# Delays in a planner's order: key turns, a block's loads, and one product of a two-layer encoder

## The chip, the cores and the metric

The kernel runs on one core of a Trainium2 chip. The metric is the device time of one execution in microseconds (us), and versions are compared by the median of several executions. The engines are TensorE (PE, with its weight loads, PEld, beside it), VectorE (DVE), ScalarE (ACT), GpSimd (POOL) and the queue engine SyncE (SP), which issues nearly all transfers between HBM and the on-chip memory.

## The reference

Two groups of 512 tokens of width 1024 go through the same two layers, each added to its input, and a last normalization. Shortened:

```python
def trunk(x):
    x = x + diff_attention(rms_norm(x, norm_g[0]))    # 8 heads, two softmaxes each
    x = x + bidir_retention(rms_norm(x, norm_g[1]))   # 8 heads, forward and backward
    return rms_norm(x, final_norm_g)

def diff_attention(h):
    q, k, v, gate = split(h @ w_in)                   # 1024 x 8192
    q, k = rotary_half(q) * d ** -0.5, rotary_half(k)
    p = softmax(q @ k.T)                              # two per head
    o = (p[0] - lam * p[1]) @ v
    return (rms_norm(o, subln_g) * (1 - lambda_init) * silu(gate)) @ w_out

def bidir_retention(h):
    q, k, v, gate = split(h @ w_in)                   # 1024 x 6144
    q, k = retention_rotate(q), retention_rotate(k) * dk ** -0.5
    o = retention(q, k, v, g_fwd) + flip(retention(flip(q), flip(k), flip(v), g_bwd))
    return (rms_norm(o, subln_g) * silu(gate)) @ w_out
```

## The kernel before

**Stages.** The order of the work is: input norms and operands; the products of the first layer's input projection; attention, head by head and group by group, with the output projection in between; the second layer's norm and input projection (about 1038 to 1535 us of the profile); retention with its output projection and the last norm (to the end). Each matrix product is split into a high and a low part of fp32r and done in three passes (`PASSES`). Projections go to DRAM and are read back as whole blocks by the stage that follows.

**The projection's products.** The projections use seven products for each 2 x 2 block of a matrix, P1 to P7, in the order P1, P2, P5, P6, P3, P7, P4. A `Unit` is a set of columns with its seven products. For units of kind "pair" (queries, keys, gates) a product is one piece of work of 12 matmuls with 512 columns; for "wide" units (values) it is four pieces of 12 matmuls with 256 columns. P1 of the next unit comes between P7 and P4 of a unit. In the very last unit P4 is the last product of the projection; before it come P4 of the unit before and P7. `projections` is a generator, and `step(proj, n)` lets it add n more products. The right-hand operands of the products lie in slots (`B_SLOT`) that later stages take over: T3 (slots 20 to 23, used by P7) and T4 (24 to 27, used by P4) become the x tiles `xN` of the first and of the second group.

**Turns.** In the second layer's key units (four of them, two heads each) the rotated keys are also needed transposed. `turn`, called from `rot_done`, does it for each of the two groups and for i = 0, 1: four PE transposes into the only PSUM bank of the tag "tp" (line 685), and two DVE multiplications by the decay powers out of that bank (line 688). The first set (i = 0) reads the difference that line 670 makes, the second (i = 1) the sum of line 672. That is four sets a unit, sixteen in all. The turned keys go to DRAM as `kt_d`.

**Retention.** A block is a head and a group. `fetch2(b)` loads a block's queries and keys, values, turned keys and gate. `score2` makes two chunks' scores (line 1221), `state2` a chunk's state (line 1244), `av2` the sums of scores with values (line 1263) and of queries with states (line 1267); after a norm on ACT and POOL comes `turn_o` (line 786) and `gate_o` (line 792). `ahead(b, n)` gives the four pieces state, score, state, score of a block; those of block b + 1 are listed beside the sums of block b. `out_step` is the output projection (line 860) with its addition to x (line 865), and for the last head `final_norm`: a square for the row's norm (`square`, line 883), a multiplication by the gain (line 1285), and, once the row's factor is there (`row_norm`, lines 890 to 893), a scaling (lines 1292 and 1293) and a store.

**The planner.** All of this only lists operations, each with its engine, an estimated cost and what it reads and writes. `Plan.arrange` then simulates the engines and fixes the order of every engine's instructions; the instructions carry no times. An operation becomes known when its predecessors have started or ended (`preds` count to the end, `order` to the start). On PE the operation with the smallest `place` among those that are ready goes next, as long as it is at most `WINDOW` = 24 places ahead of the first one that is not done; on other engines the one with the smallest `late`, the time by which its followers want it. Loads are held back until 15 us before their lateness (`AHEAD`). An issue of a DMA costs 0.5 us in the model. `Plan.issue` runs this three times, each time with the PE starts of the time before, and keeps the order with the shortest span. The parameter `wait` of an operation adds to its place on PE: the transposes of `turn` have 4.

```python
        place = {n: i + ops[n][7] for i, n in enumerate(pe)}
...
        def known(n):
            for e in ops[n][0]:
                heapq.heappush(soon[e], (ready[n], n))
```

Of the kernel before, what the change touches and what calls it, by code (L numbers as in the profile page):

```python
# [15 lines left out]
P = 128  # L16
# [5 lines left out]
NG = 2  # L22
# [44 lines left out]
class Plan:  # L67
# [2 lines left out]

    WINDOW = 24
    AFTER = dict(PE=0.2, DVE=0.12, ACT=0.13, POOL=0.13, SP=0.0)
    SAME = dict(PE=0.0, DVE=.11, ACT=.11, POOL=0.0, SP=0.0)
    BUS = 380.0
    AHEAD = 15.0

    def __init__(self):
        self.rings, self.state, self.ops = {}, {}, []

    def op(self, eng, cost, fn, r=(), w=(), lands=0.0, kb=0, load=False, wait=0):  # L80

        n = len(self.ops)
        costs = eng if isinstance(eng, dict) else {eng: cost}
        preds, order = set(), set()
        for keys, writes in ((r, False), (w, True)):
            keys = [key if isinstance(key, tuple) else (key, None) for key in keys]
            keys += [(k.also, part) for k, part in keys if isinstance(k, Buf) and k.also]
            for thing, part in keys:  # L90
                parts = self.state.setdefault(id(thing), {"thing": thing})
                if isinstance(thing, Buf):
                    if thing.nth + thing.bufs < len(thing.ring):
                        late = thing.ring[thing.nth + thing.bufs]
                        assert late.first is None, f"{thing.tag} {thing.nth} is used after its place was taken"
                    if thing.first is None:
                        assert writes, f"{thing.tag} is read before it is written"
                        thing.first = n
                        if thing.nth:
                            before = thing.ring[thing.nth - 1].first  # L100
                            assert before is not None, f"{thing.tag}: places are taken out of turn"
                            order.add(before)
                        if thing.nth >= thing.bufs:
                            preds.update(thing.ring[thing.nth - thing.bufs].users)
                    elif thing.first != n:
                        order.add(thing.first)
                    thing.users.append(n)
                for q, entry in parts.items():
                    if q == "thing" or not (part is None or q is None or q == part):
                        continue  # L110
                    if entry[0] is not None:
                        preds.add(entry[0])
                    if writes:
                        preds.update(entry[1])
                if writes:
                    if part is None:
                        for q in [q for q in parts if q != "thing"]:
                            del parts[q]
                    parts[part] = [n, []]
                else:  # L120
                    parts.setdefault(part, [None, []])[1].append(n)
        preds.discard(n)
        order -= preds
        self.ops.append((costs, fn, sorted(preds), sorted(order), lands, kb, load, wait))
        return n

    def arrange(self, starts):
# [20 lines left out]
            at = min(recent[n] + 20.0, now + 10.0) if at is None else at - cost  # L148
            late[n] = min(at, starts[n]) if "PE" in costs else at
        pe = [n for n in range(n_ops) if "PE" in ops[n][0]]  # L150
        place = {n: i + ops[n][7] for i, n in enumerate(pe)}
        left = [len(op[2]) + len(op[3]) for op in ops]
        ready = [0.0] * n_ops
        done = [False] * n_ops
# [7 lines left out]

        def known(n):
            for e in ops[n][0]:
                heapq.heappush(soon[e], (ready[n], n))

        for n in range(n_ops):
            if not left[n]:
# [74 lines left out]
def trunk_kernel(  # L243
# [104 lines left out]
    def run(gen):  # L348
        for _ in gen:
            pass  # L350
# [6 lines left out]
    def act(n, fn, r, w):  # L357
        plan.op("ACT", 0.1 + 0.00083 * n, fn, r, w)

    def dve(n, fn, r, w):  # L360
        plan.op("DVE", 0.07 + 0.00104 * n, fn, r, w)

    def pool(n, fn, r, w):
        plan.op("POOL", 0.15 + 0.0024 * n, fn, r, w)
# [7 lines left out]
                nc.vector.tensor_scalar(out(), src(), scale(), None, op0=ALU.mult)  # L372
        plan.op(dict(DVE=0.07 + each * n, ACT=0.1 + 0.00092 * n), 0, fn, r, w)

    def pe(cost, fn, r, w, wait=0):
        plan.op("PE", cost, fn, r, w, wait=wait)

    def dma(out, in_, r, w, kb, eng=None):

        q = eng or nc.sync  # L380
        plan.op("SP" if eng is None else "ACT", 0.5, lambda: q.dma_start(out(), in_()), r, w, lands=2.0 + kb / 200.0,
                kb=kb, load=any(isinstance(k[0] if isinstance(k, tuple) else k, Buf) for k in w))

    def hi_of(n, dst, src, r, w):
# [247 lines left out]
    def rot_done(dst, tab, scaled, turned=None):  # L632
# [44 lines left out]
        def turn(g, *r):  # L677
            h, to = turned
            out = [m_t("kt"), m_t("kt")]
            for i in range(2):  # L680
                tp = bank("tp", "ktp")

                def fn(i=i, tp=tp):
                    for t in range(NT):
                        nc.tensor.transpose(tp[:, t * P:(t + 1) * P], r[i][:, t * P:(t + 1) * P], ident.t)
                pe(0.44, fn, [r[i], ident], [tp], 4)
                for j in range(2):
                    dve(256, lambda i=i, j=j, tp=tp: nc.vector.tensor_tensor(
                        out[j].t.rearrange("p (t i c) -> p t i c", t=NT, i=2)[:, :, i, :],
                        tp.t.rearrange("p (t j c) -> p t j c", t=NT, j=2)[:, :, j, :],  # L690
                        powers[:, 0, h + j, :].unsqueeze(2).broadcast_to([P, NT, 64]), op=ALU.mult),
                        [tp, powers], [(out[j], i)])
            for j in range(2):
                o, k = os_t(), out[j]
                hi_of(S, lambda o=o, k=k: o[:, 0, :], lambda k=k: k.t, [k], [(o, 0)])
                lo_of(S, lambda o=o: o[:, 1, :], lambda k=k: k.t, lambda o=o: o[:, 0, :], [k, (o, 0)], [(o, 1)])
                dma(lambda j=j: to[h + j, g].rearrange("a p c -> p a c"), lambda o=o: o.t.bitcast(F32),
                    [o], [to[h + j, g]], 512)
# [126 lines left out]
            if len(todo) > lag:  # L825
                todo.pop(0)()

    def new_xN(src):
        for g in range(NG):
            for t in range(NT):  # L830
                x = xN[g, t] = slot(20 + 4 * g + t, [P, D], F32)
                dma(lambda x=x: x.t, lambda g=g, t=t: src(g, t)[0], src(g, t)[1], [x], 512)

    def out_weights(w, h, i):
        r = raw_t([P, 2, S])
# [309 lines left out]
    for i in range(N + 3):  # L1145
        at(scores, i, N)
        at(row_max, i, N)
        at(exps, i, N)
        at(combine, i, N)
        if i < 3:  # L1150
            step(proj, 1)
        if i == 2:
            run(proj)
            new_xN(lambda g, t: (xs[g][0, t * P:(t + 1) * P, :], []))
        fill(1, LAG)
        at(transp, i - 1, N)
        fill(1, LAG)
        at(turned, i - 3, N)
        at(av, i - 2, N)
        if i < N and i % 4 == 2 and i > 4:  # L1160
            nh, ng = tiles[i][0:2]
            if ng == 1 and nh + 1 < NH:
                fetch1(nh + 1, 0)
            elif ng == 0 and nh > 0:
                fetch1(nh, 1)
# [19 lines left out]
    def fetch2(b):  # L1185
        h, g = blocks[b]
        for which in range(2):
            qk[b, which] = load_qk((qk_d[1, which, h - h % 2, g], h % 2), (4, 14)[which] + b % 2, (16, 32)[which])
        vt[b] = load_v(v_d[1, h, g], 2 * (b % 2), 0)
        t = kts[b] = slot(6 + b % 2, [P, 2, S], F32R, 16)  # L1190
        dma(lambda: t.t.bitcast(F32), lambda: kt_d[h, g].rearrange("a p c -> p a c"), [kt_d[h, g]], [t], 512)
        sg[b] = load_sg(g_d[1, h, g])

    def decay(h):

# [82 lines left out]
    def final_norm(g, t, i, half, n, key, end):  # L1278
# [3 lines left out]
        if c0 == 0:  # L1282
            zs.append(e_t("z"))
        z = zs[-1]
        dve(n, lambda: nc.vector.tensor_tensor(z[:, c0:c0 + n], half, fin[i][:, c0:c0 + n], op=ALU.mult),
            [key, fin[i]], [(z, c0)])
        if not end:
            return
        r = row_norm(g, t)
        for i, z in enumerate(zs):  # L1290
            plan.op(dict(DVE=0.07 + 0.00058 * S, ACT=0.1 + 0.00092 * S), 0, lambda e, z=z: (
                nc.scalar.activation(z.t, z.t, AF.Copy, scale=r.t) if e == "ACT" else
                nc.vector.tensor_scalar(z.t, z.t, r.t, None, op0=ALU.mult)), [z, r], [z])
            dma(lambda i=i: ys[g][0, t * P:(t + 1) * P, i * S:(i + 1) * S], lambda z=z: z.t, [z], [], 256,
                nc.scalar if n < S and i == 0 else None)
        zs.clear()
# [4 lines left out]

        (state2 if n % 2 == 0 else score2)(b, (1, 0, 0, 1)[n])

    fetch2(0)
    fetch2(1)
    decay(0)
    fin = [const([P, S], n) for n in ("cos", "sin")]
    for i in range(2):
# [5 lines left out]
    N2 = len(tiles2)  # L1314
    wsn.clear()
    owed.clear()
    for j in range(NT):
        ahead(0, j)
        step(proj, 1)
    new_xN(lambda g, t: (x_d[g, t][:], [x_d[g, t]]))  # L1320
    for i in range(N2 + 2):
        if i < N2:
            b, t = tiles2[i]
# [3 lines left out]
                ahead(b + 1, t)  # L1327
            fill(1, LAG)
            av2(b, t)
            if t == 3 and b + 2 < NB:  # L1330
                fetch2(b + 2)
        fill(1, LAG)
# [67 lines left out]
```

## Time and profile before

| | |
|---|---|
| Time, median of 3 runs | 1845.91 us (1844.75 to 1852.18) |
| Time of the profiled execution | 1847.08 us |
| Its span, first to last instruction | 1845.3 us |
| PE busy | 1810.7 us, 98% of the span |
| PEld, DVE, ACT, POOL busy | 1573.3, 1465.4, 955.7, 144.7 us |
| Mean DMA rate | 175 GB/s |

A row of the timeline has the start and the duration in us, engine, line and operation, the tiles written and read, the shape, the count of like instructions merged into it and, in brackets, how long the engine was idle before it and for whom it waited. A row of the waits has the waiting engine, tile and line, whom it waited for, the total in us, the number of times and the longest. A row of a group has its busy time and the mean of one instruction in ns. "q" behind an engine's name is its queue or sequencer. A PE matmul's end is modelled, since matmuls overlap.

### The profile page before, as it was taken

What the parts mean: (1) busy time and instruction counts of PE and PEld (TensorE: products, weight loads), DVE (VectorE), ACT (ScalarE), POOL (GpSimd) and SP (SyncE); (2) the same over time, 40 slices, a digit from 0 to 9 for tenths busy, and PEclk for the clock granted to TensorE, in tenths of its full rate; (3) what the DMA queues carried; (4) which work ended last, traced back from release to release, by engine and by line L of the source; (5) the groups of instructions that cost most, each with busy time, mean ns of one, the idle gap of its engine ahead of it and who ended that gap; (6) DMA issues with size and microseconds to landing.
All of it is one profiled execution on the core that took longest, in us unless ns stands there. A gap on an engine that the chain in (4) does not pass through costs nothing.

```text
span 1845.3 us, 28198 instructions
## 1 busy us (share of the span) xinstructions
PE 1810.7 (98%) x10407; PEld 1573.3 (85%) x10407; DVE 1465.4 (79%) x2514; ACT 955.7 (52%) x1999; POOL 144.7 (8%) x373
## 2 busy tenths in 40 slices
PE   7999999999999999999999999999999999999998
PEld 5789889898898888888888888989898888888887
DVE  7986878887877788888888897868786867777778
ACT  7734434433443565555555874444444446555556
POOL 1000000000000011111111200000000001111112
PEclk9999999999999999999999999999999999999999
DMA  4365536454544684444453434646355559556462
GB/s 161 104 184 158 149 106 219 137 170 151 170 138 160 235 302 164 179 183 164 164 177 124 160 105 136 217 145 192 132 187 167 172 193 367 204 195 228 179 221 92
DMA packets 158547, 322.56 MB, mean 175 GB/s; under 512 B 12597, under 2 KB 72649, under 8 KB 158409
## 3 DMA queue, kind: packets, MB, share of 16 engines
q1 hardware_dynamic: 158080, 320.43, 51.7%
q8 instruction: 81, 1.33, 0.3%
q14 instruction: 58, 0.47, 0.1%
q10 hardware_dynamic: 328, 0.34, 0.1%
HBM read 203.28 MB, written 117.44 MB: 174 GB/s over the span
## 4 chain that ended last, share of the span: by engine, by line
PE 86%; DVE 7%; DMA 4%; ACT 1%; issue 1%; SPq 1%; POOL 0%; POOLq 0%; DVEq 0%; ACTq 0%
PE pj L576 20%; PE pj L860 18%; PE sc L576 10%; PE pj L583 8%; PE o L576 5%; PE o L1108 5%; PE sc L1056 5%; PE sc L583 4%; PE o L1263 2%; PE tp L1092 1%; PE o L786 1%; DMA raw<-in_ret_w_in_dram 1%; DVE ws L388 1%; PE o L583 1%; PE sc L1221 1%
## 5 line engine op out<-in xcount | busy, mean ns | idle before, releaser
L860 PE MATMUL pj<-ws,arena 128*128 128x512 f32 x1542 | 401.7, 398 | 0.3 <-ACT m L370 0.3
L860 PEld LDWEIGHTS pj<-ws,arena 128*128 128x128 f32 x1542 | 275.5, 188 | 49.7 <-ACT m L370 0.5
L576 PE MATMUL pj<-b,ws 128*128 128x512 f32 x1200 | 294.3, 392 | 1.5 <-DVE e L613 1.1
L576 PEld LDWEIGHTS pj<-b,ws 128*128 128x128 f32 x1200 | 224.5, 188 | 50.9 <-issue 1.5
L576 PE MATMUL sc<-arena,ws 128*128 128x512 f32 x960 | 232.3, 392 | 1.1 <-DVE arena L444 1.1
L576 PEld LDWEIGHTS sc<-arena,ws 128*128 128x128 f32 x960 | 180.2, 188 | 40.6 <-DVE arena L444 1.3
L865 DVE TENSOR_TENSOR b<-pj,b 128x512 f32<-128x512 f32 (+1 forms) x257 | 175.8, 684 | 49.0 <-PE pj L860 48.5
L388 DVE TENSOR_TENSOR ws<-st,ws 128x512 fp32r<-128x512 f32 (+1 forms) x192 | 147.7, 774 | 73.2 <-ACT ws L385 60.4
L388 DVE TENSOR_TENSOR ws<-raw,ws 128x512 fp32r<-128x512 f32 (+1 forms) x172 | 147.0, 860 | 73.5 <-ACT ws L385 58.7
L385 ACT CAST ws<-st 128x512 fp32r<-128x512 f32 (+1 forms) x192 | 132.1, 692 | 133.1 <-PE pj L576 39.3
L576 PE MATMUL pj<-arena,ws 128*128 128x512 f32 x720 | 177.3, 392 | 0.0
L385 ACT CAST ws<-raw 128x512 fp32r<-128x512 f32 (+1 forms) x172 | 130.7, 766 | 69.6 <-PE o L576 38.3
L770 POOL TENSOR_SCALAR css<-css 128x1 f32<-128x1 f32 x128 | 32.5, 254 | 1630.3 <-ACT o L768 916.3
L576 PEld LDWEIGHTS pj<-arena,ws 128*128 128x128 f32 x720 | 134.6, 188 | 28.9
L605 ACT COPY c<-pj 128x512 f32<-128x512 f32 x112 | 65.3, 584 | 132.8 <-PE pj L576 87.9
L576 PE MATMUL o<-arena,ws 128*128 128x512 f32 x480 | 117.5, 396 | 1.8 <-DVE e L444 1.8
L583 PE MATMUL pj<-ws,b 128*128 128x256 f32 x960 | 116.9, 276 | 0.0
L583 PEld LDWEIGHTS pj<-ws,b 128*128 128x128 f32 x960 | 113.2, 188 | 0.7
L576 PEld LDWEIGHTS o<-arena,ws 128*128 128x128 f32 x480 | 90.6, 190 | 21.5 <-ACT ws L385 2.0
L1072 ACT ACTIVATE b<-sc,nm 128x512 f32<-128x512 f32 x128 | 87.8, 687 | 39.9 <-DVE nm L1064 39.8
L385 ACT CAST arena<-og 128x256 fp32r<-128x256 f32 x128 | 51.8, 405 | 105.7 <-DVE og L792 105.7
L1108 PE MATMUL o<-arena 128*128 128x256 f32 x768 | 106.1, 288 | 0.0
(176 smaller groups left out, 3000.3 us busy)
## 6 DMA issues: line engine op xcount, KB each, us to landing
qk<-os SPq DMA_DIRECT2D x192, 256.0 KB, 3.8
arena<-qk SPq DMA_DIRECT2D x96, 512.0 KB, 6.2
raw<-in_da_w_in_dram SPq DMA_DIRECT2D x64, 512.0 KB, 5.0
v<-os SPq DMA_DIRECT2D x64, 512.0 KB, 4.8
arena<-v SPq DMA_DIRECT2D x64, 512.0 KB, 4.1
raw<-in_ret_w_in_dram SPq DMA_DIRECT2D x48, 512.0 KB, 4.6
os<-g SPq DMA_DIRECT2D x32, 512.0 KB, 8.6
g<-e SPq DMA_DIRECT2D x48, 256.0 KB, 4.9
```

Source lines behind the costliest of these rows:

```text
L385: act(n, lambda: nc.scalar.copy(dst(), src()), r, w)
L388: dve(n, lambda: nc.vector.tensor_tensor(dst(), src(), hi().bitcast(F32), op=ALU.subtract), r, w)
L576: nc.tensor.matmul(ps.t, a[u][0]()[:, k, :], bt[k][:, v, :], start=(opens and k == 0 and i == 0), stop=(k == 3 and i == 2), skip_group_che ...
L583: nc.tensor.matmul(ps[:, (t % 2) * 256:(t % 2) * 256 + 256], bt[k][:, v, t * P:(t + 1) * P], a[u][0]()[:, k, :], start=(opens and t % 2 == ...
L605: act(S, lambda c=c, ps=ps: nc.scalar.copy(c.t, ps.t), [ps], [c])
L770: pool(60, lambda: nc.gpsimd.tensor_scalar(ss.t, ss.t, 256 * SUB_EPS, None, op0=ALU.add), [ss], [ss])
L860: nc.tensor.matmul(ps[:, here], o[a][:, e, t * P:(t + 1) * P], u[b][:, e, here], start=(p == 0 and m == 0), stop=(m == 5), skip_group_chec ...
L865: dve(n, lambda half=half, here=here: nc.vector.tensor_tensor(half, ps[:, here], half, op=ALU.add), [ps if parts == 1 else (ps, p), part], ...
L1056: nc.tensor.matmul(s.t, q[:, a, t * P:(t + 1) * P], k[:, b, :], start=(n == 0), stop=(n == 2))
L1072: act(840, lambda j=j, s=s, m=m: nc.scalar.activation(p[:, j, :], s.t, AF.Exp, bias=m.t, accum_out=sm[:, j:j + 1]), [s, m], [(p, j), (sm, j)])
L1108: nc.tensor.matmul(o[:, 0:256], aT[:, a, j * P:(j + 1) * P], v[b][:, j, :], start=(n == 0), stop=(n == 11))
L1263: nc.tensor.matmul(o[:, 0:256], a_[:, u, j * 256 + tt * P:j * 256 + (tt + 1) * P], v_[v][:, 2 * c + j, :], start=(j == 0 and i == 0), stop ...
```

## The change

- `wait` becomes a time: an operation is offered to its engine `wait` us after it is ready in the model, and its place on PE is that of its position. The transposes of `turn` get 5 (us) for 4 (places).
- A DMA issue costs 0.62 us in the model for 0.5.
- While `plan.first` is set, each load gets an `order` entry: it may be issued only after that operation has been. It is set to the load of the first block's keys while the second block's loads are listed.
- The last product of the second layer's projection (P4 of the last unit) is listed after `av2(0, 0)` and after the first state piece of block 1, for before the first block's last scores; the x loads of each group directly behind the product that frees their slots. In the first layer the x loads are split in the same way; the products there keep their order.
- At the end, the gain multiplication of the last tile's first half is offered 1.0 us late, and the scaling of the tile before it 0.75 us late.

```diff
-    def op(self, eng, cost, fn, r=(), w=(), lands=0.0, kb=0, load=False, wait=0):
+        self.first = None
+
+    def op(self, eng, cost, fn, r=(), w=(), lands=0.0, kb=0, load=False, wait=0.0):
...
+        if load and self.first is not None:
+            order.add(self.first)
...
-        place = {n: i + ops[n][7] for i, n in enumerate(pe)}
+        place = {n: i for i, n in enumerate(pe)}
...
-                heapq.heappush(soon[e], (ready[n], n))
+                heapq.heappush(soon[e], (ready[n] + ops[n][7], n))
...
-    def dve(n, fn, r, w):
-        plan.op("DVE", 0.07 + 0.00104 * n, fn, r, w)
+    def dve(n, fn, r, w, wait=0.0):
+        plan.op("DVE", 0.07 + 0.00104 * n, fn, r, w, wait=wait)
...
-        plan.op("SP" if eng is None else "ACT", 0.5, lambda: q.dma_start(out(), in_()), r, w, lands=2.0 + kb / 200.0,
+        plan.op("SP" if eng is None else "ACT", 0.62, lambda: q.dma_start(out(), in_()), r, w, lands=2.0 + kb / 200.0,
...
-                pe(0.44, fn, [r[i], ident], [tp], 4)
+                pe(0.44, fn, [r[i], ident], [tp], 5)
...
-    def new_xN(src):
-        for g in range(NG):
-            for t in range(NT):
-                x = xN[g, t] = slot(20 + 4 * g + t, [P, D], F32)
-                dma(lambda x=x: x.t, lambda g=g, t=t: src(g, t)[0], src(g, t)[1], [x], 512)
+    def new_xN(g, src):
+        for t in range(NT):
+            x = xN[g, t] = slot(20 + 4 * g + t, [P, D], F32)
+            dma(lambda x=x: x.t, lambda t=t: src(t)[0], src(t)[1], [x], 512)
...
-        if i < 3:
-            step(proj, 1)
-        if i == 2:
-            run(proj)
-            new_xN(lambda g, t: (xs[g][0, t * P:(t + 1) * P, :], []))
+        for n, when in enumerate((0, 1, 2)):
+            if i == when:
+                step(proj, 1)
+                if n:
+                    new_xN(n - 1, lambda t, n=n: (xs[n - 1][0, t * P:(t + 1) * P, :], []))
...
+        keys = len(plan.ops) - 1
         vt[b] = load_v(v_d[1, h, g], 2 * (b % 2), 0)
...
+        return keys
...
+        final = (g, t) == (NG - 1, NT - 1)
         dve(n, lambda: nc.vector.tensor_tensor(z[:, c0:c0 + n], half, fin[i][:, c0:c0 + n], op=ALU.mult),
-            [key, fin[i]], [(z, c0)])
+            [key, fin[i]], [(z, c0)], 1.0 if final and i == 0 else 0.0)
...
-                nc.vector.tensor_scalar(z.t, z.t, r.t, None, op0=ALU.mult)), [z, r], [z])
+                nc.vector.tensor_scalar(z.t, z.t, r.t, None, op0=ALU.mult)), [z, r], [z], wait=0.75 if (g, t) == (NG - 1, NT - 2) else 0.0)
...
-    fetch2(0)
+    plan.first = fetch2(0)
     fetch2(1)
+    plan.first = None
...
-    for j in range(NT):
-        ahead(0, j)
-        step(proj, 1)
-    new_xN(lambda g, t: (x_d[g, t][:], [x_d[g, t]]))
+    ahead(0, 0)
+    step(proj, 1)
+    ahead(0, 1)
+    ahead(0, 2)
+    step(proj, 1)
+    new_xN(0, lambda t: (x_d[0, t][:], [x_d[0, t]]))
+    ahead(0, 3)
...
             av2(b, t)
+            if i == 0:
+                step(proj, 1)
+                new_xN(1, lambda t: (x_d[1, t][:], [x_d[1, t]]))
```

More of the change, by code (lines that the diff above doesn't have):

```diff
@@ L72 @@
     AFTER = dict(PE=0.2, DVE=0.12, ACT=0.13, POOL=0.13, SP=0.0)
-    SAME = dict(PE=0.0, DVE=.11, ACT=.11, POOL=0.0, SP=0.0)
+    SAME = dict(PE=0.0, DVE=0.11, ACT=0.11, POOL=0.0, SP=0.0)
     BUS = 380.0
@@ L373, in evac, with pe @@
         plan.op(dict(DVE=0.07 + each * n, ACT=0.1 + 0.00092 * n), 0, fn, r, w)
-    def pe(cost, fn, r, w, wait=0):
+    def pe(cost, fn, r, w, wait=0.0):
         plan.op("PE", cost, fn, r, w, wait=wait)
```

## The prediction

> **What bounds the kernel now.** I read the page first, then the busy time of each engine in stretches of 50 us, then who TensorE waited for, then the timeline at those places.
>
> ```profile
> span 1845.3 us, 28198 instructions
> PE 1810.7 (98%) x10407; PEld 1573.3 (85%) x10407; DVE 1465.4 (79%) x2514; ACT 955.7 (52%) x1999; POOL 144.7 (8%) x373
> ```
>
> TensorE (PE) is busy for 1810.7 of 1845.3 us, and the change leaves its arithmetic as it is. So no edit can bring more than the 34.6 us in which PE is idle, plus what the modelled ends hide. The stretches say where these are (columns: PE, PEld, DVE, ACT, POOL busy, clock, DMA share, GB/s).
>
> ```profile
> 0.00:50.00 50.00, 36.29 (x166) 30.09 (x166) 36.97 (x62) 34.80 (x59) 9.09 (x20) 0.97 0.42 149
> 50.00:100.00 50.00, 48.52 (x211) 39.23 (x210) 44.69 (x74) 33.52 (x59) 0.00 (x0) 1.00 0.44 135
> ...
> 1150.00:1200.00 50.00, 47.10 (x361) 44.45 (x360) 41.14 (x65) 22.15 (x37) 0.00 (x0) 1.00 0.61 201
> ...
> 1250.00:1300.00 50.00, 48.47 (x373) 45.97 (x372) 41.12 (x65) 22.32 (x36) 0.00 (x0) 1.00 0.62 200
> ...
> 1350.00:1400.00 50.00, 48.04 (x371) 45.50 (x370) 41.20 (x65) 22.19 (x36) 0.00 (x0) 1.00 0.62 201
> ...
> 1450.00:1500.00 50.00, 48.45 (x373) 45.90 (x372) 42.26 (x67) 22.79 (x38) 0.00 (x0) 1.00 0.57 190
> 1500.00:1550.00 50.00, 48.44 (x259) 41.02 (x258) 28.40 (x53) 29.06 (x65) 3.45 (x10) 1.00 0.82 296
> ```
>
> The start loses 13.7 + 1.5 us. Four stretches 100 us apart lose 2.9, 1.5, 2.0 and 1.5 us: 7.9 us, once for each of the four units of keys in the second layer. The entry into the retention stage (1500 to 1550) loses 1.6 us. The granted clock is 1.00 in all but the first stretch, so these are gaps and nothing else. PE's waits name the four stretches:
>
> ```profile
> PE tp L685 <- DVE m L670: 4.5, 4, 1.9
> PE tp L685 <- DVE m L688: 3.5, 4, 1.0
> ```
>
> Eight of the sixteen sets of key transposes (L685) wait for VectorE (DVE), 8.0 us in all. The kernel's order is written by its planner; the planner put these sets where its model had the data just ready, and the chip's DVE was later than the model.
>
> **Turns of the keys: five microseconds instead of four places.** One unit on the timeline of PE, and of DVE:
>
> ```profile
> 1145.12 5.63 PE L583 MATMUL pj<-ws,arena 128*128 128x256 f32 x48
> 1152.68 0.66 PE L685 MATMUL tp<-ident,m 128*128 128x128 f32 x4 [1.92 <-DVE m L670]
> 1153.09 3.01 PE L576 MATMUL pj<-b,ws 128*128 128x512 f32 x12
> 1155.93 0.60 PE L685 MATMUL tp<-ident,e 128*128 128x128 f32 x4
> ...
> 1159.35 0.66 PE L685 MATMUL tp<-ident,m 128*128 128x128 f32 x4
> ...
> 1165.07 0.66 PE L685 MATMUL tp<-ident,e 128*128 128x128 f32 x4 [0.97 <-DVE m L688]
> ```
>
> ```profile
> 1151.94 0.68 DVE L670 TENSOR_TENSOR m<-m,m 128x512 f32<-128x512 f32 x1
> ...
> 1163.67 0.42 DVE L688 TENSOR_TENSOR m<-tp,powers 128x256 f32<-128x256 f32 x1
> ...
> 1164.60 0.42 DVE L688 TENSOR_TENSOR m<-tp,powers 128x256 f32<-128x256 f32 x1
> ```
>
> The first set of a unit waits for the rotated key (L670), the fourth for the single PSUM bank "tp" that the third set's evacuation (L688) frees. In the new plan a set may be taken only 5.0 us after its inputs are ready by the model; other products go in the meantime, and the instruction itself has no delay in it. The longest lateness seen is 1.92 us, so 5.0 covers every one of the eight. The matmuls in the gap are there: behind the first set stand the unit's P4 (12 matmuls, 2.75 us) and the next unit's P2.
>
> A gap is longer than its row says, because the end before it is modelled:
>
> ```profile
> 136.37 5.44 PE sc L583 x48
> ```
>
> ```profile
> L583 PE MATMUL pj<-ws,b 128*128 128x256 f32 x960 | 116.9, 276 | 0.0
> ```
>
> 48 such matmuls follow each other in 5.44 us, 113 ns each, while one is drawn 276 ns long. So each gap hides up to 163 ns: 8 x 0.163 = 1.3 us. The term is 8.0 + 1.3 = **9.3 us**; bounds: 4.6 (half of the sets still wait) and 9.3.
>
> What is late next: the four sets now follow each other at 5 us and more, because "tp" is one bank and the wait counts from its release. From set to evacuated set takes 0.41 us to the next PE instruction (1152.68 to 1153.09), 0.75 for the two L688 and some 0.15 of handing over, so 6.3 us a set. The first would go at 1150.76 (1152.68 less the 1.92) + 5.0 = 1155.8, the fourth at 1155.8 + 3 x 6.3 = 1174.7 instead of 1165.1. Until then the rotated key keeps one of eight "e" buffers, which the second sum of the wide unit's P7 takes next. That product ends at about 1150.8 + 2.75 (P4) + 5 x 5.44 (P2, P5, P6, P3, P7) + 3 x 0.41 = 1182. 7 us are left, so I cost this at nothing; gone, it is rival C. The stores of the turned keys move with the sets on SP's queue, and they are read only after 1508.
>
> **Second block's loads behind the first one's keys.**
>
> ```profile
> 1508.40 2.38 SPq L381 DMA_DIRECT2D arena<-v  x4
> ...
> 1513.63 0.93 SPq L381 DMA_DIRECT2D arena<-qk  x2
> ...
> 1516.13 0.61 SPq L381 DMA_DIRECT2D arena<-kt  x1
> ...
> 1519.00 0.32 SPq L381 DMA_DIRECT2D arena<-qk  x1
> ```
>
> ```profile
> arena<-v SPq DMA_DIRECT2D x64, 512.0 KB, 4.1
> ```
>
> ```profile
> 1519.00:1529.00 10.00, 9.30 (x47) 7.70 (x45) 3.91 (x6) 4.50 (x8) 0.00 (x0) 1.00 1.03 400
> ```
>
> ```profile
> 1529.05 1.65 PE L1221 MATMUL sc<-arena 128*128 128x256 f32 x12 [0.75 <-DMA arena<-qk]
> 1531.40 3.03 PE L576 MATMUL pj<-b,ws 128*128 128x512 f32 x12
> ...
> 1538.84 0.44 PE L786 MATMUL o<-ident,on 128*128 128x128 f32 x2 [0.24 <-ACT on L780]
> 1539.85 0.97 PE L1263 MATMUL o<-arena 128*128 128x256 f32 x6 [0.57 <-DVE og L792]
> ```
>
> The load at 1519.00 is the first block's keys; it can't be issued earlier, since its place is freed by a product. The DMA engines are full (share 1.03, 400 GB/s), so it lands only when PE takes it up at 1529.05, after a wait of 0.75. Ahead of it in the queue are two of the four v loads, one of the two qk loads and the kt load of 1516.13 that belong to the second block. At 400 GB/s one of 512 KB takes 1.31 us, four 5.2 us. Behind the keys they let these land at about 1524, and the wait goes, since PE gets there only after P4 of the unit before the last: **0.75 us** (bounds 0 and 0.75). On SP these four, the second block's keys and its gate load stand behind the new order and nothing else; who waits for them is the state product of the second block, and that is rival B.
>
> Here a page speaks against the edit: by the Trainium skill, "DMA: Bandwidth & Descriptors", section "Where 436 GB/s comes from", transfers between HBM and SBUF are bound near 358 GB/s on a core. By that rate the four loads are 5.9 us (an estimate) and what is held back comes later still; the 400 GB/s of the row, loads and stores together, is above that figure, and the measurement decides.
>
> **The last product behind the first block's sums.** P4 of the last unit (1531.40, 2.75 us) goes from before the first block's first sums (L1263, L1267) to behind them. It then runs while the norm of these sums is on ACT and POOL, where PE now waits 0.24 + 0.57 = **0.8 us** (bounds 0 and 0.8). What it covered before, the way from the first scores to the first sums, keeps P7 (another 2.75 us) and three small products. The x loads of the first group come only after P7, those of the second only after P4; both are free of other claims, and their first use (1542 and later) is far enough.
>
> **The end.**
>
> ```profile
> 1837.69 0.68 DVE L1285 TENSOR_TENSOR e<-b,cos 128x512 f32<-128x512 f32 x1
> 1838.29 0.41 DVE L865 TENSOR_TENSOR b<-pj,b 128x256 f32<-128x256 f32 x1
> ```
>
> ```profile
> 1838.43 0.71 ACT L1292 ACTIVATE e<-e,rsf 128x512 f32<-128x512 f32 x1
> 1839.04 0.40 ACT L883 ACTIVATE c<-b 128x256 f32<-128x256 f32 x1
> ```
>
> The last addition (L865) waits behind a multiplication (L1285), the last square (L883) behind a scaling (L1292). Both in the way get a delay in the plan (1.0 and 0.75 us) and go behind. The last square can start at 1838.43: **0.6 us** (bounds 0 and 0.6); what moves back has until 1840.9, when the row's factor is there.
>
> **A DMA issue costed at 0.62 instead of 0.5 us.** This touches the whole plan. The row at 1513.63 has two issues in 0.93 us, so 0.5 is nearer the chip where nothing waits; 0.62 errs to the late side. It has no row of its own. From below, 2 us gained in the first 100 us, whose 15.2 idle us are mostly the first loads and norms; from above, 4 us lost, two new gaps of the longest size seen (1.92). I take 0, being nearest to the many stretches without a gap. The other edits of text (defaults, the first layer's loads in two calls) change no operation.
>
> **The sum.** 9.3 + 0.75 + 0.8 + 0.6 = 11.5 us. The profiled execution took 1847.1 us, 1.8 beyond its span and 1.2 above the median of the runs, 1845.9. So 1847.1 - 11.5 = 1835.6 for such an execution, and **1834.4 us** for the median.
>
> **Rivals.** *A, the replan gives part back.* Lateness of DVE moves with the sets, or the new issue cost makes gaps elsewhere. For: no stretch is without some work whose place rests on the model. Against: DVE has 7.7 to 8.9 idle us in each of the four stretches. Half of the sets waiting takes 4.6 us from the gain: 1839.0; with the 4 us of new gaps 1843.0.
>
> *B, held-back loads.* The second block's loads leave DMA time unused before 1519 and all that queues behind is later, by up to the 5.2 us of four loads. Against: PE has two products P4 and P7 and the first block's sums to run. It would give 1834.4 + 5.2 = 1839.6. By the 358 GB/s of the Trainium skill's page named above it would be 1834.4 + 5.9 = 1840.3, an estimate.
>
> *C, slower: the delayed sets hold the buffers.* The planner runs three rounds and takes the starts of one as the lateness of the next, so a set that starts later makes DVE's work for it less urgent, and its 5 us may be added once more. For four sets that is 20 us, the fourth at 1194.7; PE would wait for the "e" buffer from 1182 + 2.75 (one product stands between). It decides from a slip of 10 us on. The price is 10 us a unit, 40 in all: 1874. Against: the planner sees the buffers and may take up to 24 places of later products.
>
> *D, nothing changes.* The plan of the retention entry and of the turns comes out with the gaps elsewhere: 1845.9.
>
> **How the numbers follow.** The forecast has 0.58, A 0.17, B 0.10, C 0.10, D 0.05. The forecast's own range is 1830 (11.5 + 2 from the start + 2 that modelled ends hide in the other terms) to 1837. A measurement of this kernel can tell about 0.5%, 9.2 us, from no change: 1836.7 to 1855.1. A, B and D lie inside: 0.32. The range that should hold 8 in 10 takes in A, B and D, 1830 to 1846, and leaves out C and a rest below.
>
> **What would show it.** The waits of L685 should be gone from PE's list and the four stretches full to within 0.3 us; the four sets of a unit 5 us or more apart, the fourth some 10 us later. The scores at about 1524 should not wait for the qk load; P4's 12 matmuls should follow the first L1267. The last square should start where the last addition ends. Gaps before L576 or L583 near 1182, or a wait for kt or v in the second block's state product, would show C or B. If the gaps of L685 remain, the main term is wrong.

## The result and the profile after

| | before | changed |
|---|---|---|
| Median of 21 runs | 1847.7 us | 1837.37 us |
| Range of the runs | 1843.75 to 1852.46 | 1834.39 to 1846.27 |
| Span of the profiled execution | 1845.3 us | 1834.8 us |
| Ratio | | 0.9951, interval 0.9940 to 0.9962 |

By the ratio, which is that of the means, the change is faster by 0.49% (0.38 to 0.60), 9.1 us of 1847.7; the medians lie 10.3 us apart. The forecast was 11.5 us, 0.62%. The time lies in the range of 1830 to 1846 that should hold 8 in 10, and 0.4 us above the narrower 1830 to 1837. The forecast took 0.5% for the least that a measurement can tell from no change; the interval here, a tenth of a per cent to each side, tells this 0.49% from none. The page of the changed kernel begins:

```profile
span 1834.8 us, 28223 instructions
PE 1809.7 (99%) x10407; PEld 1574.7 (86%) x10407; DVE 1469.8 (80%) x2515; ACT 953.0 (52%) x1998; POOL 149.4 (8%) x373
```

PE's work is the same (10407 matmuls), and its idle time fell from 34.6 to 25.1 us. The stretches of the changed kernel that answer to those shown before (PE, PEld, DVE, ACT, POOL busy, clock, DMA share, GB/s):

```profile
0.00:50.00 50.00, 36.29 (x165) 29.91 (x166) 36.97 (x62) 34.90 (x59) 9.14 (x20) 0.97 0.42 149
...
1050.00:1100.00 50.00, 49.36 (x233) 40.77 (x232) 49.11 (x82) 33.28 (x59) 4.98 (x2) 1.00 0.21 69
1150.00:1200.00 50.00, 50.00 (x377) 47.52 (x376) 39.52 (x66) 22.87 (x39) 0.00 (x0) 1.00 0.67 211
1250.00:1300.00 50.00, 50.00 (x371) 47.33 (x370) 37.97 (x62) 23.44 (x39) 0.00 (x0) 1.00 0.64 200
1350.00:1400.00 50.00, 50.00 (x370) 47.33 (x369) 36.72 (x60) 22.16 (x37) 0.00 (x0) 1.00 0.67 209
1450.00:1500.00 50.00, 50.00 (x367) 47.13 (x367) 37.84 (x61) 22.39 (x39) 0.00 (x0) 1.00 0.59 191
1500.00:1550.00 50.00, 49.68 (x289) 43.45 (x288) 32.12 (x61) 30.23 (x73) 6.35 (x14) 1.00 0.96 359
```

The four stretches with the key units are full, where 7.9 us were idle. The entry to retention has 0.3 us idle for 1.6. The stretch from 1050 has 0.6 us of new idle time; before it was full:

```profile
1050.00:1100.00 50.00, 50.00 (x235) 41.28 (x234) 49.76 (x82) 36.40 (x63) 2.01 (x2) 1.00 0.25 79
```

One key unit on the timeline of PE, changed kernel:

```profile
1155.50 0.60 PE L689 MATMUL tp<-ident,m 128*128 128x128 f32 x4
...
1162.77 0.60 PE L689 MATMUL tp<-ident,e 128*128 128x128 f32 x4
...
1170.03 0.60 PE L689 MATMUL tp<-ident,m 128*128 128x128 f32 x4
...
1177.54 0.60 PE L689 MATMUL tp<-ident,e 128*128 128x128 f32 x4
```

The four sets (line 689 now) have no wait. They stand 7.3 to 7.5 us apart, and the fourth goes 12.5 us later than before. The entry to retention on the same timeline:

```profile
1517.57 0.87 PE L1226 MATMUL sc<-arena 128*128 128x256 f32 x6
...
1523.14 0.84 PE L1268 MATMUL o<-arena 128*128 128x256 f32 x6
1523.82 0.50 PE L1272 MATMUL o<-b,arena 128*128 128x256 f32 x3
1524.16 2.91 PE L580 MATMUL pj<-b,ws 128*128 128x512 f32 x12
...
1529.14 0.44 PE L790 MATMUL o<-ident,on 128*128 128x128 f32 x2 [0.32 <-ACT on L784]
```

The last product (12 matmuls at 1524.16) follows the first sums, the first scores (line 1226) wait for nothing, and the first turn of sums still waits 0.32 us. The new gap, in the start of the second layer:

```profile
1059.07 2.31 PE L580 MATMUL o<-arena,ws 128*128 128x512 f32 x9 [0.64 <-DVE e L448]
```

And the end, on ACT, in the changed kernel:

```profile
1827.34 0.63 ACT L886 ACTIVATE c<-b 128x512 f32<-128x512 f32 x1 [0.45 <-DVE b L868]
...
1828.37 0.40 ACT L886 ACTIVATE c<-b 128x256 f32<-128x256 f32 x1
...
1828.77 0.71 ACT L1298 ACTIVATE e<-e,rsf 128x512 f32<-128x512 f32 x1
```

The square that answers to the one at 1827.34 was before:

```profile
1837.40 0.63 ACT L883 ACTIVATE c<-b 128x512 f32<-128x512 f32 x1 [0.45 <-DVE b L865]
```

In the changed kernel the last square starts 1.03 us after that one (1827.34 to 1828.37); before it was 1.64 (1837.40 to 1839.04). The scaling stands behind it now. From that same square to the end of the span it is 7.4 us, before 7.9, so 0.45 us are left of the 0.6.

### The profile page after: what moved, and what is told of

Its sections match the earlier page's. It is cut to its first block, busy times and chain, and to the rows that moved or that the text cites. A ratio compares the mean times of both kernels' runs of the same rounds, so it can differ in the third digit from the quotient of the medians.

```text
span 1834.8 us, 28223 instructions
## 1 busy us (share of the span) xinstructions
PE 1809.7 (99%) x10407; PEld 1574.7 (86%) x10407; DVE 1469.8 (80%) x2515; ACT 953.0 (52%) x1998; POOL 149.4 (8%) x373
## 4 chain that ended last, share of the span: by engine, by line
PE 92%; DVE 3%; DMA 2%; ACT 2%; POOL 1%; issue 1%; SPq 0%; POOLq 0%; DVEq 0%; ACTq 0%
PE pj L580 21%; PE pj L863 18%; PE sc L580 11%; PE pj L587 10%; PE o L580 6%; PE o L1111 5%; PE sc L587 5%; PE sc L1059 5%; PE o L587 2%; PE o L1268 2%; PE tp L1095 1%; PE o L790 1%; PE o L1272 1%; PE sc L1226 1%; PE tp L1249 1%; DMA arena<-qk 1%
```

## Experiments

Theory: the waits before the key transposes carry the gain, the other edits about 2 us. Rival: the replan, by the issue cost above all, gives part back or carries part itself; and the delayed sets hold buffers.

**1. The turns' rule alone** (kernel before, with):

```diff
-        place = {n: i + ops[n][7] for i, n in enumerate(pe)}
+        place = {n: i for i, n in enumerate(pe)}
-                heapq.heappush(soon[e], (ready[n], n))
+                heapq.heappush(soon[e], (ready[n] + ops[n][7], n))
-                pe(0.44, fn, [r[i], ident], [tp], 4)
+                pe(0.44, fn, [r[i], ident], [tp], 5)
```

> The kernel before, with the turns' rule alone changed: wait counts as time, 5 us for 4 places. If the eight waits before the key transposes are the main term, they go from TensorE's list (8.0 us by the rows, 9.3 with what the modelled ends hide), the four stretches at 1150, 1250, 1350 and 1450 us are full, and the time is about 9 us below the kernel before (0.995). If the replan gives part back, half of it stays: 4 to 5 us (0.9975). If the delayed sets hold the buffers, new gaps stand before products of the wide unit near 1182 us.

Measured: 1837.95 us against 1845.55 for the kernel before, ratio 0.9957 (0.9941 to 0.9973), span 1834.6. No wait before a key transpose is left; of the waits in the second half PE's list keeps these:

```profile
PE o L1263 <- DVE og L792: 0.6, 1, 0.6
...
PE o L786 <- ACT on L780: 0.2, 1, 0.2
```

This edit alone gives 7.9 us by the ratio (5.0 to 10.9). That is most of the whole's 9.1 (7.0 to 11.1); by the time the two are not told apart, so what the other edits add is not shown by it.

**2. Everything but the turns' rule** (the changed kernel, the sets again with 4 places and no time):

```diff
-        place = {n: i for i, n in enumerate(pe)}
+        place = {n: i + (4 if ops[n][7] == 5 else 0) for i, n in enumerate(pe)}
-                heapq.heappush(soon[e], (ready[n] + ops[n][7], n))
+                heapq.heappush(soon[e], (ready[n] + (0 if ops[n][7] == 5 else ops[n][7]), n))
```

> The changed kernel with the turns' old rule (4 places, no time). By the main term the gaps return and the time is within 2 to 3 us of the kernel before (0.998 to 0.999), since the retention entry and the end keep some 2.2 us. If the other edits carry more than that, it stays at 0.997 or below.

Measured: 1840.66 us, ratio 0.9971 (0.9958 to 0.9984), 5.4 us below the kernel before, more than the 2 to 3 expected. Together with experiment 1 that is 13 us, where both give 9. The waits say part of why:

```profile
PE tp L689 <- DVE m L692: 2.4, 3, 1.1
...
PE tp L689 <- DVE m L674: 1.5, 3, 1.0
```

3.9 us before the transposes instead of 8.0: another edit had already shortened what the turns' rule takes away. One more thing to know here: with 0 places for 4 the planner writes the same program, instruction by instruction, for this kernel and for the kernel before. The old parameter did nothing, so the new rule puts 5 us where there was no delay at all.

**3. The issue cost alone** (kernel before, with):

```diff
-        plan.op("SP" if eng is None else "ACT", 0.5, lambda: ...
+        plan.op("SP" if eng is None else "ACT", 0.62, lambda: ...
```

> The kernel before, with 0.62 us for a DMA issue in the model and nothing else. With the turns' old rule the changed kernel kept only about 5 us of gaps before the key transposes, where the kernel before has 9.3 (start to start). If the issue cost is what shortened them, this kernel has about 5 us there too, the new gap of 0.8 us near 1058 us, and is about 3 us faster than before (0.998). If the shortening came from the moves at the entry to retention, the gaps are 9 us as before and the time is the same (1.000).

Measured: 1844.36 us, ratio 0.9994 (0.9978 to 1.001), which is 1.1 us gained (4.1 gained to 1.8 lost). PE's waits:

```profile
PE tp L685 <- DVE m L688: 2.6, 3, 1.3
...
PE tp L685 <- DVE m L670: 1.4, 3, 0.7
...
PE o L786 <- ACT on L780: 1.0, 2, 0.7
```

The waits before the transposes are 4.0 us, where the two executions of the kernel before have 8.0 and 6.9 (experiment 10), so the issue cost alone shortens them. The time hardly moves, though the interval does not exclude the 3 us expected; a wait of 0.7 for ACT at the end of the first layer (1035 us) is new. The gap near 1058 is not there. So that gap comes from this edit together with others, not from it alone.

**4. The old issue cost in the changed kernel** (0.62 back to 0.5).

> The changed kernel with 0.5 us for a DMA issue in the model instead of 0.62. If the issue cost only reshuffles where nothing waits, time and gaps equal the changed kernel's within 1 us (0.995). If 0.62 is what made the new gap near 1058 us (0.8 us), that gap goes; if it carries part of the gain, the time rises by 2 us or more.

Measured: 1840.68 us (1835.81 to 1843.77), ratio 0.9958 (0.9942 to 0.9974), span 1834.0. The gap near 1058 is gone, one of 0.5 us for ACT is there at 1030, and two waits for keys in retention (1560 and 1578 us) of 0.5 together. Not told apart from the changed kernel.

**5. Two microseconds for five.**

```diff
-                pe(0.44, fn, [r[i], ident], [tp], 5)
+                pe(0.44, fn, [r[i], ident], [tp], 2)
```

> The changed kernel with 2 us for the turns' wait. In the changed kernel the third set of each unit goes only 1.2 to 1.5 us after its data, the first 3.1 to 3.3: the model was 3.5 to 3.8 and 1.8 us early. If that lateness is what counts, with 2 us the third set waits again (up to 1.5 us in each of the four units, 2 to 6 us in all) and the first hardly; the time is 2 to 5 us above the changed kernel (0.997). If any delay of the order of the longest old wait (1.92 us) is enough, no gap returns (0.995).

Measured: 1836.59 us, ratio 0.9945 (0.9927 to 0.9963), and no wait before a transpose; the sets of the first unit stand 4.5 to 4.7 us apart. The reading behind the expectation (that the third set would be late by 1.5 us) was wrong: with another wait the planner sets DVE's order anew too (it is not the changed kernel's), and the distance in one plan is not the lateness in another.

**6. Ten microseconds for five.**

> The changed kernel with 10 us for the turns' wait: the fourth set of a unit goes some 20 us later, past the point (1182 us) at which the wide unit needs the buffer that the key holds. If the held buffers matter, PE waits before products of the wide unit or the next one, up to 10 us a unit, and the time is above the changed kernel by 5 us or more (0.998 or higher). If the planner finds other work, the four stretches stay full and the time equals the changed kernel's (0.995).

Measured: 1843.17 us, ratio 0.9979 (0.9965 to 0.9992), slower in every run (1841.85 to 1845.36) than any of experiment 5 (1835.97 to 1836.85). The fourth set of the first unit goes at 1189.48, 24.4 us later than in the kernel before. Waits that are new or longer:

```profile
PE sc L580 <- DVE arena L448: 2.9, 2, 1.6
PE pj L587 <- DVE e L617: 2.1, 4, 0.9
...
PE tp L1095 <- DVE arena L392: 1.1, 1, 1.1
```

One wait a unit, four times, of a wide unit's product for a sum (line 617): 0.23, 0.18, 0.95 and 0.74 us. On DVE at the third of them:

```profile
1388.63 0.69 DVE L539 TENSOR_TENSOR st<-raw,raw 128x512 f32<-128x512 f32 x1 [2.09 <-DMA raw<-in_ret_w_in_dram]
...
1390.69 0.75 DVE L692 TENSOR_TENSOR m<-tp,powers 128x256 f32<-128x256 f32 x2
...
1391.36 0.68 DVE L617 TENSOR_TENSOR e<-pj,c 128x512 f32<-128x512 f32 x1
```

The sum stands behind the evacuation of the late set (line 692) and behind a weight load for which DVE sat idle 2.09 us. In all four units of this kernel's program the sum writes the very "e" buffer that the fourth set has just read, so it can't come before the set: that is the buffer that rival C named. But it costs 0.5 us a unit and not 10, and it goes with the load: DVE was idle for it 1.36, 1.32, 2.09 and 1.87 us in the four units. Of the other two rows, the 1.1 (654 us) and 1.3 of the 2.9 (1072 us) lie in stages that have no turns: the plan changed there as well.

**7. The entry as before** (the changed kernel without `plan.first` and with the products and x loads where they were).

> The changed kernel with the entry to retention as before: no order between the two blocks' loads, the last product and the x loads where they were. If the entry is worth what its waits say (0.75 for the keys, 0.8 for the sums, and another wait for keys of 0.4 to 0.9 near 1567 us), it is 1.5 to 2.5 us slower than the changed kernel: 0.996 of the kernel before. If held-back loads cost as much as they bring, it equals the changed kernel.

Measured: 1837.89 us, ratio 0.9956 (0.994 to 0.9972), span 1835.1; not told apart from the changed kernel by time. Two rows of PE's list:

```profile
PE o L790 <- ACT on L784: 1.0, 2, 0.7
...
PE o L1268 <- DVE og L796: 0.6, 1, 0.6
```

Of the 1.0, 0.73 lies at the end of the first layer (1035 us). At the first sums there are 0.24 and 0.57, the 0.8 of the kernel before: these waits are back. No wait for keys is in the list, although the loads stand as before. The gap near 1058 is gone, so it needs the edits at the entry too.

**8. Load order old, product moved** (the changed kernel without these lines):

```diff
-    plan.first = fetch2(0)
+    fetch2(0)
     fetch2(1)
-    plan.first = None
```

> The changed kernel without the order between the two blocks' loads; the last product stays behind the first sums. If the held loads are what lets the first block's keys land in time, the first scores (line 1226) wait 0.2 to 0.9 us for them near 1518 to 1522 us. If the moved product covers the landing anyway, no wait for keys is seen there.

Measured in one execution: 1838.22 us, span 1836.4. PE's timeline at the entry:

```profile
1521.16 1.57 PE L1226 MATMUL sc<-arena 128*128 128x256 f32 x12
1522.57 0.86 PE L1249 MATMUL tp<-arena 128*128 128x256 f32 x6
1523.44 3.02 PE L580 MATMUL pj<-b,ws 128*128 128x512 f32 x12
1526.30 0.87 PE L1268 MATMUL o<-arena 128*128 128x256 f32 x6
...
1530.96 0.44 PE L790 MATMUL o<-ident,on 128*128 128x128 f32 x2 [0.97 <-ACT on L784]
1531.97 0.97 PE L1268 MATMUL o<-arena 128*128 128x256 f32 x6 [0.57 <-DVE og L796]
```

The scores wait for no keys, yet the last product (1523.44) stands ahead of the first sums (line 1268), although it is listed behind them. A likely reason, argued and not shown, is that without the load order the model has the keys late and the planner fills the time with the product. The two waits at the sums are 1.5 us.

**9. Product old, load order kept.**

> The changed kernel with the last product before the first sums again, the load order kept. If the product is what covers the norm of the first sums, the two gaps at the first turn of sums and at the next sums return (0.4 and 0.74 us, start to start) in place of the one of 0.5; the first scores do not wait for keys.

Measured in one execution: 1840.28 us, span 1838.5, with the waits at the sums:

```profile
1532.46 0.44 PE L790 MATMUL o<-ident,on 128*128 128x128 f32 x2 [0.88 <-ACT on L784]
1533.47 0.96 PE L1268 MATMUL o<-arena 128*128 128x256 f32 x6 [0.57 <-DVE og L796]
```

1.45 us, and no wait of the first scores. Neither edit alone takes these waits away (1.5 and 1.45 us, more than the 0.8 of the kernel before and of experiment 7, which has neither); both together leave 0.32 or none. The rest of this span's 3.7 us above the changed kernel lies partly in waits of the first layer and of the second layer's start (654, 1035 and 1072 us), as in experiment 6.

**10. Both kernels once more, and an issue cost of 0.7.**

> The kernel before once more, for its gaps on the same chip as the others. If the gaps before the key transposes are set by the order and not by the run, they are 8 to 9.5 us again, start to start, and the entry to retention has the same waits (0.9, 1.1 and 0.9 us at 1528, 1538 and 1567 us).

> The changed kernel once more, on the chip of the others: 0.995 of the kernel before, no gap before the key transposes, the gap near 1058 us and one of 0.5 us at the first turn of sums near 1529 us again; the wait for keys near 1767 us (0.2 to 0.4 us) may come and go with the run.

> The changed kernel with 0.7 us for a DMA issue in the model. In its order TensorE's start of the second layer is that of the kernel before (no wait near 1058 us), the turns and the entry to retention are those of the changed kernel. If the gap near 1058 us (0.8 us) comes from the order that 0.62 gave, it goes, no other comes, and the time is 0.5 to 1 us below the changed kernel. If the issue cost itself is worth something, the time moves by more.

The kernel before, span 1842.8, 2.5 us below its first profile. Its waits:

```profile
PE tp L685 <- DVE m L688: 4.1, 4, 1.5
PE tp L685 <- DVE m L670: 2.8, 4, 0.8
...
PE o L1263 <- DVE og L792: 0.6, 1, 0.6
PE o L786 <- ACT on L780: 0.2, 1, 0.2
PE sc L1221 <- DMA arena<-qk: 0.2, 1, 0.2
```

6.9 us before the transposes instead of 8.0, the same 0.8 at the sums, and no wait for the first block's keys: the 0.2 is later (1736 us). The changed kernel, span 1834.9, 1836.51 us, ratio 0.9959 (0.9945 to 0.9972), has no wait at the first sums at all and again the gap near 1059.

With 0.7 us for an issue PE's order at the start of the second layer is that of the kernel before, and the gap near 1059 went, but another came:

```profile
1069.87 2.33 PE L580 MATMUL sc<-arena,ws 128*128 128x512 f32 x9 [0.65 <-DVE arena L448]
```

Three waits for keys in retention (1560, 1578 and 1749 us) are there as well, 1.5 us together. Measured: 1835.66 us, ratio 0.9949 (0.9936 to 0.9961), not told apart from the changed kernel. No version is shown to be better than it.

**All runs from one instruction on.** The first transposes of the second layer's norm (line 986, later 989) are the same instruction in PE's order in every run, 4702 matmuls from the end. They start between 1036.3 and 1038.6 us whatever the edits. From there to the end, in three of the runs:

```profile
1037.47:1845.30 807.83, 789.13 (x4703) 692.56 (x4701) 621.81 (x1071) 420.82 (x881) 64.16 (x151) 1.00 0.53 182
```

```profile
1036.52:1834.70 798.18, 788.73 (x4703) 695.11 (x4701) 623.65 (x1070) 418.61 (x880) 63.40 (x151) 1.00 0.53 184
```

```profile
1037.42:1834.80 797.38, 788.20 (x4703) 694.37 (x4701) 624.92 (x1072) 416.55 (x880) 68.21 (x151) 1.00 0.54 185
```

These are the kernel before, experiment 1 and the changed kernel. One profile for each entry of this table:

| Kernel | us from there to the end |
|---|---|
| before, two executions | 807.8, 806.1 |
| changed, two executions | 797.4, 796.9 |
| 1: turns' rule alone | 798.1 |
| 2: all but the turns' rule | 801.8 |
| 3: issue cost alone | 804.2 |
| 4: changed, old issue cost | 796.4 |
| 5 and 6: 2 us, 10 us | 797.9, 801.7 |
| 7: changed, entry as before | 797.1 |
| 8 and 9: one half of the entry's edits | 799.5, 799.9 |
| 10: issue cost 0.7 | 798.6 |

The turns' rule alone takes off 8.0 to 9.7 us of the whole's 8.7 to 10.9. The entry's edits together take off nothing that shows, and either half of them without the other takes 2 to 3 us more in these single executions.

## Why the prediction was right, and where its sizes were off

**Direction and main term.** The waits of the key transposes went, all of them, and experiment 1 gives 7.9 us for them alone. The sum had 9.3. The second profile of the kernel before has 6.9 + 8 x 0.163 = 8.2: the term differs by about 1 us between two executions, and the prediction had seen the one with more. The mechanism held: sets that the plan places some us behind their data find it there, and other products fill the time.

**The sets' spacing and the buffers.** The sets stand 7.3 to 7.5 us apart for 6.3; the fourth went 12.5 us later, where 9.6 was worked out, and no buffer held PE up. At 10 us of wait the fourth set went past 1182 and rival C's buffer was in the way, as its reasoning had it. Its price did not follow: other products stand between, and PE waits 0.5 us a unit.

**Second block's loads.** The 0.75 was mis-sized: it is a wait of one execution. In the second profile of the kernel before, and in experiments 1 and 7 with the old load order, the first scores wait for no keys. What this edit does is in the plan: with it the planner leaves the last product behind the sums, without it not (experiment 8). The prediction took the two edits for independent terms; in the waits they are one, worth about what the sums' term said, 0.5 to 0.8 us. In time not even that is shown: with the entry as before (experiment 7) the second layer is as short, and the gap near 1059 is gone. Rival B, a cost of held-back loads, was not seen in PE's list at the entry. Whether it has a part in the waits for keys at 1560 to 1583 us (0.5 to 1.1 us in experiments 2, 4, 9 and 10) is open; the kernel before has 0.42 there too, which the sum left out.

**The end.** 0.6 forecast, 0.45 measured: the last square came earlier by 0.6, but from it to the last scaling it took 2.11 us (1828.37 to 1830.48) where it had been 1.94 (1839.04 to 1840.98). Not all of the 0.45 need be the edit's: in experiment 3, which has the old end, the stretch from the same square to the end is 7.6 us, where the kernel before has 7.9.

**The issue cost.** Taken as 0 with bounds of 2 gained and 4 lost. It has two effects. It shortens the waits that the turns' rule removes in any case to some 4 us (experiments 2 and 3), so that this part counts for nothing in the whole. With the entry's edits it leaves the new gap of 0.64 us, 0.8 with the hidden 0.163, near 1059. This is rival A's new gap elsewhere, at a fifth of its price of 4 us.

**The sum with these sizes.** 8.2 + 0 + 0.8 + 0.45 - 0.8 = 8.7 us, against 9.1 measured (7.0 to 11.1). The other 0.4 is inside what the interval allows, and the terms below 1 us are sizes of waits, not shown one by one in the time. From the second layer's first transposes on, the two profiles of each kernel lie 8.7 to 10.9 us apart. The error of the prediction was to take every wait of a single execution at its full size, and the replan at nothing.

**Left open.** The spans of experiments 2 and 3 differ by 3.2 us, 2.4 of it in the second layer, while PE's waits there are 5.7 and 5.6 us; what the modelled ends hide of it was not followed. So it is not shown why experiment 2 gains 5.4 us and experiment 3 only 1.1 with the same waits left. The edits at the end were not run alone. Which edits of the plan make the gaps at 654, 1035, 1059 and 1072 us come and go was not followed further.

## What to carry to other kernels

Here an order was fixed ahead by a model, and operations that the model placed just in time waited on the chip. A margin of the size of the longest such wait (2 us for 1.92) took all of these waits away, 5 us were no better, and 10 brought other waits. Edits to such a planner need not add up: before crediting one with a gap, look whether another already moves it. A parameter of the planner may do nothing at all, as the 4 places did: look whether the order changes without it. And read a wait of under a microsecond from two executions before it becomes a term.

## What the runs showed of the hardware

Two executions of one order differed in their span by 2.5 us (1845.3 and 1842.8), with a wait for a load of 0.75 us in one that the other did not have, and with 8.0 and 6.9 us of waits of TensorE for VectorE at the same eight places. Loads and stores together ran at 400 GB/s for 10 us (1519 to 1529 us of the kernel before), with a busy share of 1.03 of the sixteen DMA engines.

The granted clock of TensorE was 0.50 for about 3 us near 32 us in the first profile of the kernel before and in both of the changed kernel, and 1.00 there in all other profiles. From 32 to 35 us, in the first and in the second profile of the kernel before:

```profile
32.00:35.00 3.00, 3.00 (x8) 2.33 (x8) 2.24 (x5) 1.01 (x2) 0.00 (x0) 0.50 0.03 5
```

```profile
32.00:35.00 3.00, 3.00 (x15) 2.47 (x14) 3.00 (x6) 1.41 (x3) 0.00 (x0) 1.00 0.02 5
```

The columns are those of the stretches above. 8 matmuls stand in these 3 us in the one and 15 in the other. Spans of single profiles differ by this too, so the experiments are compared above from the second layer on.
